# Odd attention's values product over pairs of token tiles in split parts, with the head norm taken over partitions

## The chip, the cores and the metric

The kernel runs on one core of a Trainium2 chip. The metric is the time of one execution on the device in microseconds. Five engines have instruction queues of their own: TensorE (PE), VectorE (DVE), ScalarE (ACT), GpSimd (POOL) and SyncE (SP, which issues transfers here). PE's weight loads are listed as PEld.

## The reference

A bidirectional encoder of two layers is applied to a prompt of 256 tokens and a sample of 512 tokens, width 1024, with shared weights. The even layer has neighbourhood and grouped-query attention, the odd layer differential attention with 8 heads; an MLP follows each. The change lies in the odd layer:

```python
def diff_attention(q, k, v, lam):
    ...
        s = jnp.einsum('bqhcd,bkhcd->bhcqk', q_blk, kk).astype(jnp.float32) * scale
        p = jax.nn.softmax(s, axis=-1)
        a = (p[:, :, 0] - lam * p[:, :, 1]).astype(v.dtype)
        return jnp.einsum('bhqk,bkhe->bqhe', a, v)
...
            o = diff_attention(qc, kc, vc, lam)
            o = rmsnorm(o, subln_g[j], SUBLN_EPS) * (1.0 - lam_init)
            x = x + o.reshape(B, T, DIFF_WIDTH) @ w_out_o[j]
```

For each head there are two score maps (64 features each); the second softmax, times lambda, is taken from the first. The difference multiplies values of 128 features, and the result is normalized over those 128 features for each token.

## The kernel before

Both requests lie side by side as 768 tokens, six tiles of 128; tiles 0 to 3 are the sample (512 keys), tiles 4 and 5 the prompt (256 keys). Large products are done in split form: each f32 operand is written as a high part in the type F32R and the remainder as a low part (`wsplit`, `halve`; ACT writes the high part, DVE subtracts), and three F32R products, high-high, high-low and low-high, are added in PSUM.

Odd attention is a pipeline of two strands that share the PE queue. The first is a chain of projection steps: `proj_v` (values of two heads, tokens in the partitions) and `proj_qk` (queries and keys of one head, then the rotary products on DVE `t`, L697, the sum on POOL `rope_o`, L705 and L706, and a transpose on PE with split evacuation, `put_T`), and at the end `out_proj`. One step is six matmuls over 256 columns, in `out_proj` three over 512 and three over 256. The second strand is 48 attention units, one for each head `h` and token tile `t` (`diff_unit`), with four parts:

- `f_s`: six score matmuls into two PSUM tiles (L278), for each map the maximum `m` on DVE (L727) and the exponential `de` on ACT (L729), then on DVE the reciprocals `ri`, the factor `cf`, and the weighted sum of both maps (L734), not yet divided by the first map's sum.
- `f_t`: transposes of that sum on PE (L288), copied to SBUF by DVE and ACT in turn (L292, L294).
- `f_v`: the values product in plain f32, tokens in the partitions (L744); `od` on ACT divides by the first map's sum; ACT squares with a sum over the free axis (`odq`, L749), DVE makes the mean `ss`, POOL takes the power -0.5 (`rn`, L752), DVE multiplies (`o_tok`, L754).
- `f_o`: a PE transpose `otp` (L299) and a copy by ACT into the head's tile `do`, features in the partitions.

`attention` and `ramp` set the order in which the strands are written down: the units of head h lie between given steps of the chain, 36 steps for a full head, and in unit i come `f_s(i)`, half of the steps, `f_o(i-2)`, `f_v(i-1)`, the other half, `f_t(i)`. A scheduler that goes by priority and its own estimates of readiness sets the final order on each engine; each engine then works in that order. PSUM has three banks with the tag `mm` (projections) and five with the tag `at` (scores, transposes, values).

The even layer's grouped-query attention has a class `Values` that takes two token tiles together: transposes of both into one PSUM bank, split evacuation `gph` (L456, L457), and matmuls over 256 columns with features in the partitions.

Of the kernel before, what the change touches and what calls it, by code (L numbers as in the profile page):

```python
# [11 lines left out]
F32 = mybir.dt.float32  # L12
# [25 lines left out]
def kernel(ctx: ExitStack, tc: tile.TileContext, a: dict, y: bass.AP):  # L38
# [13 lines left out]
    nc.vector.memset(ones, 1.0)  # L52
    nhalf = cpool.tile([P, 8], F32, name="nhalf")
# [10 lines left out]
    def ps_tile(tag, name):  # L64
        return psum.tile([P, 512], F32, tag=tag, name=name, bufs=BANKS[tag])
# [214 lines left out]

    flip = [0]

    def transposed(pool, blocks, tag, name):

        n = len(blocks)
        pt = ps_tile("at", f"{name}_ps")
        for i, b in enumerate(blocks):
            nc.tensor.transpose(out=pt[:, i * P : (i + 1) * P], in_=b, identity=ident)  # L288
        sb = pool.tile([P, 512], F32, tag=tag, name=name)
        flip[0] ^= 1  # L290
        if flip[0]:
            nc.vector.tensor_copy(sb[:, : n * P], pt[:, : n * P])  # L292
        else:
            nc.scalar.activation(sb[:, : n * P], pt[:, : n * P], AF.Copy)  # L294
        return sb

    def o_out(o_tok, o_tile, t, gain=1.0):
        pt = ps_tile("at", "otp")[:, :P]
        nc.tensor.transpose(out=pt, in_=o_tok, identity=ident)  # L299
        nc.scalar.activation(o_tile[:, t * P : (t + 1) * P], pt, AF.Copy, scale=gain)  # L300
# [6 lines left out]
    def xo_tile(name):  # L307
        return xpool.tile([P, NT], F32, tag="xo", name=name, bufs=9)
# [335 lines left out]
    def odd_attention(xs, nm, sg, spill):  # L644
# [17 lines left out]
        def proj_v(n):  # L662
            col = wgroup("w_in_o")
            v = vs[n] = ap.tile([P, TT, 256], F32, tag="v", name=f"dv{n}", bufs=2)
            pend = []
            for t in range(TT):
                ps = ps_tile("mm" if n or t < 3 else "at", "dvp")
                yield from proj_tok(col, xs, t, ps)
                pend.append((t, ps))
                if not rts and t == 3:  # L670
                    rts.append(nm.rstd())
                while rts and pend:
                    t_, ps = pend.pop(0)
                    nc.scalar.activation(v[:, t_, :], ps[:, :256], AF.Copy, scale=rts[0][:, t_ : t_ + 1])
# [10 lines left out]
        def proj_qk(h):  # L685
            col = wgroup("w_in_o")
            d = qks[h] = [ap.tile([P, 2, NT], F32R, tag="qk", name=f"d{h}_{i}", bufs=6) for i in range(2)]
# [20 lines left out]

        def diff_unit(h, t):
            if t == 0:  # L710
                o[h] = xo_tile("do")
            d = qks[h]
            v, o_tile = vs[h // 2], o[h]
            vc = slice((h % 2) * P, (h % 2) * P + P)
# [5 lines left out]
            st = {}  # L720

            def f_s():
                es_ = []
                ss = scores("ds", nk * P, lambda i, hp, s: d[i][hp, 0, s], lambda i, hp, s: d[i][hp, 1, s], tk, ks)
                for c, s in enumerate(ss):
                    m = spool.tile([P, 1], F32, tag="m", name="m")
                    nc.vector.tensor_reduce(out=m, in_=s, axis=AX.X, op=ALU.max, negate=True)  # L727
                    e = ap.tile([P, 512], F32, tag="e", name="de", bufs=4)[:, : nk * P]
                    nc.scalar.activation(e, s, AF.Exp, bias=m, scale=1.0, accum_out=l2[:, c : c + 1])  # L729
                    es_.append(e)  # L730
                nc.vector.reciprocal(ri, l2)
                cf = spool.tile([P, 1], F32, tag="cf", name="cf", bufs=2)
                nc.vector.scalar_tensor_tensor(out=cf, in0=ri[:, 1:2], scalar=l2[:, 0:1], in1=neglam, op0=ALU.mult, op1=ALU.mult)
                nc.vector.scalar_tensor_tensor(out=es_[0], in0=es_[1], scalar=cf, in1=es_[0], op0=ALU.mult, op1=ALU.add)  # L734
                st["e"] = es_[0]

            def f_t():
                st["pt"] = transposed(ap, [st["e"][:, i * P : (i + 1) * P] for i in range(nk)], "pt", "dpt")

            def f_v():  # L740
                pt = st["pt"]
                pv = ps_tile("at", "dpv")[:, :P]
                for i in range(nk):
                    nc.tensor.matmul(pv, pt[:, i * P : (i + 1) * P], v[:, k0 // P + i, vc], start=(i == 0), stop=(i == nk - 1))  # L744
                od = ap.tile([P, P], F32, tag="od", name="od", bufs=2)
                nc.scalar.activation(od, pv, AF.Copy, scale=ri[:, 0:1])
                sq = ap.tile([P, P], F32, tag="odq", name="odq", bufs=1)
                ss = spool.tile([P, 1], F32, tag="ss", name="ss")
                nc.scalar.activation(sq, od, AF.Square, accum_out=ss)  # L749
                nc.vector.tensor_scalar(ss, ss, 1.0 / P, 1e-5, op0=ALU.mult, op1=ALU.add)  # L750
                rn = spool.tile([P, 1], F32, tag="rn", name="rn")
                nc.gpsimd.tensor_tensor(out=rn, in0=ss, in1=nhalf[:, :1], op=ALU.pow)  # L752
                st["o"] = ap.tile([P, P], F32, tag="o_tok", name="o_tok", bufs=2)
                nc.vector.tensor_scalar(st["o"], od, rn[:, 0:1], None, op0=ALU.mult)  # L754

            def f_o():
                o_out(st["o"], o_tile, t, sg[:, 0:1])

            return f_s, f_t, f_v, f_o
# [563 lines left out]
```

## Time and profile before

| what | value |
|---|---|
| median of three runs | 1723.32 us (1722.27 to 1725.19) |
| profiled execution | 1722.56 us, span 1720.8 us |
| TensorE clock granted, mean | 0.996 |
| busy over the span: PE, PEld, DVE, ACT, POOL | 99%, 94%, 78%, 52%, 21% |
| odd attention, with its projections | from 833 to 1208 us of the span |

Busy is the share of the span in which an engine executed something; it doesn't count the time in which a queue stands because its next instruction waits for another engine. Waits are listed apart, with the engine and line that ended them. The profiled execution lies 0.8 us under the median.

### The profile page before, as it was taken

The page shows a single profiled execution, that of the slowest core. Times are in us where ns is not written, and L with a number is a line of the kernel's source. Part 1 is how long each engine was busy: PE and PEld are TensorE (multiplying, and loading weights), DVE is VectorE, ACT ScalarE, POOL GpSimd, SP SyncE. Part 2 cuts the span into 40 slices and gives each one's busy share as a digit, 9 for nine tenths or more (in the row PEclk, how much of TensorE's full clock was granted, in tenths as well). Part 3 has the DMA queues.
Part 4 walks back from the last instruction along what each step waited for, and adds up shares of the span by engine and source line. Part 5 has one row for each costly group of instructions (what it writes and reads, how often), then busy time and mean ns, then how long its engine had stood idle before and what let it go on. Part 6 is the DMA issues. An engine that isn't in the chain of part 4 may idle for free. (4 is left out here: it accounts for less than half of the span.)

```text
span 1720.8 us, 28225 instructions
## 1 busy us (share of the span) xinstructions
PE 1695.1 (99%) x10844; PEld 1610.7 (94%) x10844; DVE 1344.5 (78%) x2356; ACT 897.1 (52%) x1617; POOL 355.5 (21%) x380
## 2 busy tenths in 40 slices
PE   8999999999999999999999999999999999999997
PEld 8888888899999999999999999988999999999997
DVE  8888779798887787878676776776898776878785
ACT  7765656464554544444445555555545554544442
POOL 2200000116555200000021222210246554000001
PEclk9999999999999999999999999999999999999998
DMA  5111223315544688653310111112145445996521
GB/s 172 38 47 50 68 81 107 123 53 187 169 170 163 228 311 321 218 160 131 131 50 26 50 40 33 56 59 86 50 164 175 160 169 192 331 322 228 190 90 74
DMA packets 74598, 235.42 MB, mean 137 GB/s; under 512 B 7904, under 2 KB 25056, under 8 KB 74464
## 3 DMA queue, kind: packets, MB, share of 16 engines
q1 hardware_dynamic: 52480, 186.93, 32.8%
q0 software_dynamic: 7168, 25.17, 4.3%
q10 hardware_dynamic: 14816, 21.52, 3.5%
q8 instruction: 85, 1.39, 0.3%
q14 instruction: 49, 0.40, 0.1%
HBM read 182.47 MB, written 50.33 MB: 135 GB/s over the span
## 5 line engine op out<-in xcount | busy, mean ns | idle before, releaser
L883 PE MATMUL up<-c,whi 128*128 128x384 f32 x1808 | 464.8, 338 | 1.2 <-ACT c L122 0.6
L1082 PE MATMUL dn<-th,whi 128*128 128x384 f32 x1792 | 462.2, 339 | 3.8 <-DVE th L120 3.8
L1082 PEld LDWEIGHTS dn<-th,whi 128*128 128x128 f32 x1792 | 326.9, 188 | 4.4 <-DVE th L120 4.4
L883 PEld LDWEIGHTS up<-c,whi 128*128 128x128 f32 x1808 | 328.2, 188 | 2.7 <-ACT c L122 1.3
L883 PE MATMUL up<-c,wlo 128*128 128x384 f32 x904 | 305.2, 338 | 0.0
L1082 PE MATMUL dn<-th,wlo 128*128 128x384 f32 x896 | 303.3, 339 | 0.0
L83 ACT ACTIVATE whi<-ch 128x1024 fp32r<-128x1024 f32 x88 | 93.2, 1062 | 179.4 <-PE dn L1082 164.8
L868 POOL TENSOR_TENSOR s<-wraw 128x512 f32<-128x512 f32 x60 | 93.2, 1569 | 449.5 <-DMA wraw<-in_w_up_dram 360.1
L883 PEld LDWEIGHTS up<-c,wlo 128*128 128x128 f32 x904 | 169.7, 188 | 0.0
L1082 PEld LDWEIGHTS dn<-th,wlo 128*128 128x128 f32 x896 | 168.9, 189 | 0.0
L83 ACT ACTIVATE whi<-wraw 128x1024 fp32r<-128x1024 f32 (+3 forms) x128 | 116.6, 911 | 89.0 <-PE up L883 62.9
L84 DVE TENSOR_TENSOR wlo<-ch,whi 128x1024 fp32r<-128x1024 f32 x88 | 107.1, 1223 | 56.6 <-ACT whi L83 55.2
L84 DVE TENSOR_TENSOR wlo<-wraw,whi 128x1024 fp32r<-128x1024 f32 (+3 forms) x132 | 138.9, 1052 | 14.0 <-ACT whi L83 13.8
L83 ACT ACTIVATE whi<-s 128x1024 fp32r<-128x1024 f32 x60 | 63.7, 1062 | 127.6 <-PE up L883 118.2
L200 PE MATMUL dqk<-whi,xh 128*128 128x256 f32 x384 | 114.8, 299 | 0.0
L171 POOL TENSOR_TENSOR rt<-ms,nhalf 128x6 f32<-128x6 f32 (+1 forms) x6 | 9.0, 1492 | 501.8 <-DVE ms L170 501.8
L200 PE MATMUL dqk<-whi,xl 128*128 128x256 f32 x384 | 107.4, 280 | 0.0
L200 PE MATMUL dqk<-wlo,xh 128*128 128x256 f32 x384 | 107.2, 279 | 0.0
L84 DVE TENSOR_TENSOR wlo<-s,whi 128x1024 fp32r<-128x1024 f32 x60 | 84.1, 1402 | 23.1 <-ACT whi L83 22.9
L120 DVE TENSOR_TENSOR th<-tr,th 128x1536 fp32r<-128x1536 f32 x56 | 98.2, 1753 | 3.5 <-ACT th L119 3.4
L729 ACT ACTIVATE de<-ds,m 128x512 f32<-128x512 f32 (+1 forms) x96 | 58.3, 612 | 81.3 <-DVE m L727 81.3
L891 DVE TENSOR_TENSOR z<-up,z 128x384 f32<-128x384 f32 x180 | 96.6, 550 | 1.0
(235 smaller groups left out, 3765.8 us busy)
## 6 DMA issues: line engine op xcount, KB each, us to landing
wd<-in_w_down_dram SPq DMA_DIRECT2D x84, 512.0 KB, 4.8
tr<-T SPq DMA_DIRECT2D x56, 768.0 KB, 5.7
wraw<-in_w_up_dram SPq DMA_DIRECT2D x64, 512.0 KB, 3.7
T<-t POOLq DMA_DIRECT2D x64, 384.0 KB, 3.1
T<-z ACTq DMA_DIRECT2D x32, 576.0 KB, 3.0
ch<-in_w_down_dram SPq DMA_DIRECT2D x28, 512.0 KB, 5.1
wraw<-in_w_in_o_dram SPq DMA_DIRECT2D x24, 512.0 KB, 3.6
wraw<-in_w_in_e_dram SPq DMA_DIRECT2D x16, 512.0 KB, 3.6
```

What stands on the lines that cost most here:

```text
L83: nc.scalar.activation(hi, raw, AF.Copy)
L84: nc.vector.tensor_tensor(out=lo, in0=raw, in1=hi.bitcast(F32), op=ALU.subtract)
L120: nc.vector.tensor_tensor(out=lo, in0=src, in1=hi.bitcast(F32), op=ALU.subtract)
L171: nc.gpsimd.tensor_tensor(out=rt, in0=ms, in1=nhalf[:, :n], op=ALU.pow)
L200: nc.tensor.matmul(ps[:, :256], st[:, tk], col(k, part, 0, 256), start=(k == 0 and i == 0), stop=(k == KD - 1 and i == 2))
L729: nc.scalar.activation(e, s, AF.Exp, bias=m, scale=1.0, accum_out=l2[:, c : c + 1])
L868: nc.gpsimd.tensor_tensor(out=d_, in0=x_, in1=y_, op=ALU.add)
L883: nc.tensor.matmul(ps, part[a_][:, base + k * P : base + (k + 1) * P], t[:, b_], start=start and k + i == 0, stop=stop and k == 3 and i == 2)
L891: nc.vector.tensor_tensor(out=out, in0=x_, in1=y_, op=op)
L1082: nc.tensor.matmul(ps, w[a_][:, c : c + P], th[:, b_, q], start=i + q + a_ + b_ == 0, stop=i == NG - 1 and q == ND - 1 and a_ == 1)
```

## The change

The attention units keep their places, but from `f_t` on they work on pairs of neighbouring token tiles (0 and 1, 2 and 3, 4 and 5) of a head. The weighted sum of the two maps is now fully normalized before it is transposed: ACT multiplies the second map by `cf`, DVE multiplies the first by its reciprocal sum and adds. A pair's transposes are taken in parts of two key blocks (two parts over 512 keys, one over 256), each part evacuated as a high and a low half. The values are kept as high and low halves also, and the product is done as three split products over 256 tokens, with the features in the partitions. The norm's sum over features is a product with a 128 by 128 matrix of ones, in two parts (high and low of the squares): each partition then holds the sums of all 256 tokens. DVE transposes that in blocks of 32 by 32, so that 8 columns hold the 256 sums; mean, epsilon and power are taken on these 8 columns, and a second block transpose from a broadcast spreads them again over the partitions. One DVE instruction multiplies and writes the head's output tile; the output transposes on PE are gone. The q/k tiles have four instead of six buffers.

```diff
+    ones_r = cpool.tile([P, P], F32R, name="ones_r")
+    nc.scalar.activation(ones_r, ident, AF.Copy, scale=0.0, bias=1.0)
...
-            v = vs[n] = ap.tile([P, TT, 256], F32, tag="v", name=f"dv{n}", bufs=2)
+            v = vs[n] = ap.tile([P, TT, 2, 256], F32R, tag="v", name=f"dv{n}", bufs=2)
...
-                    nc.scalar.activation(v[:, t_, :], ps[:, :256], AF.Copy, scale=rts[0][:, t_ : t_ + 1])
+                    r = rts[0][:, t_ : t_ + 1]
+                    nc.scalar.activation(v[:, t_, 0], ps[:, :256], AF.Copy, scale=r)
+                    nc.vector.scalar_tensor_tensor(out=v[:, t_, 1], in0=ps[:, :256], scalar=r, in1=v[:, t_, 0].bitcast(F32),
+                                                   op0=ALU.mult, op1=ALU.subtract)
...
+        class Values:
+            def __init__(self, h, t):
+                self.o, self.tk = o[h], slice(t * P, t * P + 256)
+                self.k0, self.nk = (0, 4) if t < 4 else (4, 2)
+                self.v, self.vc = vs[h // 2], slice((h % 2) * P, (h % 2) * P + P)
+                self.parts = list(range(0, self.nk, 2))
+                self.es, self.live, self.od = [], [], None
+
+            def turn(self):
+                if not self.parts:
+                    return
+                i = self.parts.pop(0)
+                pt = ps_tile("at", "dpt_ps")
+                for b in range(2):
+                    for t in range(2):
+                        nc.tensor.transpose(out=pt[:, b * 256 + t * P : b * 256 + (t + 1) * P],
+                                            in_=self.es[t][:, (i + b) * P : (i + b + 1) * P], identity=ident)
+                hl_ = ap.tile([P, 2, 512], F32R, tag="pt", name="dph", bufs=2)
+                nc.scalar.activation(hl_[:, 0], pt, AF.Copy)
+                nc.vector.tensor_tensor(out=hl_[:, 1], in0=pt, in1=hl_[:, 0].bitcast(F32), op=ALU.subtract)
+                self.live.append((i, hl_))
+
+            def values(self):
+                if self.parts or not self.live:
+                    return
+                pv = ps_tile("at", "dpv")[:, :256]
+                for i, hl_ in self.live:
+                    for b in range(2):
+                        for part, mv in ((0, 0), (0, 1), (1, 0)):
+                            nc.tensor.matmul(pv, self.v[:, self.k0 + i + b, part, self.vc], hl_[:, mv, b * 256 : (b + 1) * 256],
+                                             start=i + b + part + mv == 0, stop=i + b == self.nk - 1 and part == 1)
+                self.live = []
+                ...
+                nc.scalar.activation(self.ms, pv, AF.Square)
+                nc.scalar.activation(self.sq[:, 0], self.ms, AF.Copy)
+                nc.vector.tensor_tensor(out=self.sq[:, 1], in0=self.ms, in1=self.sq[:, 0].bitcast(F32), op=ALU.subtract)
+                nc.scalar.activation(self.od, pv, AF.Copy)
+
+            def out(self):
+                if self.od is None:
+                    return
+                ss = ps_tile("at", "dss")[:, :256]
+                for part in range(2):
+                    nc.tensor.matmul(ss, ones_r, self.sq[:, part], start=part == 0, stop=part == 1)
+
+                nc.vector.transpose(self.ms, ss)
+                m8 = spool.tile([P, 8], F32, tag="m8", name="m8", bufs=2)
+                nc.vector.tensor_scalar(m8, self.ms[:, 0:256:32], 1.0 / P, 1e-5, op0=ALU.mult, op1=ALU.add)
+                nc.gpsimd.tensor_tensor(out=m8, in0=m8, in1=nhalf, op=ALU.pow)
+                nc.vector.transpose(self.ms.rearrange("p (b t) -> p b t", t=32), m8[:, :, None].broadcast_to([P, 8, 32]))
+                nc.vector.scalar_tensor_tensor(out=self.o[:, self.tk], in0=self.od, scalar=sg[:, 0:1], in1=self.ms,
+                                               op0=ALU.mult, op1=ALU.mult)
+                self.od = None
...
+            if t % 2 == 0:
+                vals.append(Values(h, t))
+                del vals[:-2]
+            v = vals[-1] if t % 2 else vals[0] if len(vals) > 1 else None
+            now = vals[-1]
...
-                nc.vector.scalar_tensor_tensor(out=cf, in0=ri[:, 1:2], scalar=l2[:, 0:1], in1=neglam, op0=ALU.mult, op1=ALU.mult)
-                nc.vector.scalar_tensor_tensor(out=es_[0], in0=es_[1], scalar=cf, in1=es_[0], op0=ALU.mult, op1=ALU.add)
-                st["e"] = es_[0]
...
+                nc.vector.tensor_tensor(out=cf, in0=ri[:, 1:2], in1=neglam, op=ALU.mult)
+                nc.scalar.activation(es_[1], es_[1], AF.Copy, scale=cf)
+                nc.vector.scalar_tensor_tensor(out=es_[0], in0=es_[0], scalar=ri[:, 0:1], in1=es_[1], op0=ALU.mult, op1=ALU.add)
+                now.es.append(es_[0])
+
+            return f_s, lambda: v and v.turn(), lambda: v and v.values(), lambda: v and v.out()
```

The old `f_t`, `f_v` and `f_o` of `diff_unit` go, with their helpers `transposed` and `o_out`. The exponentials' buffers, four of one tag, become three for the first map and one for the second.

More of the change, by code (lines that the diff above doesn't have):

```diff
@@ L279, in scores @@
         return out
[L281 to L300, printed above, removed]
     def ramp(marks):
@@ L686, in proj_qk @@
             col = wgroup("w_in_o")
-            d = qks[h] = [ap.tile([P, 2, NT], F32R, tag="qk", name=f"d{h}_{i}", bufs=6) for i in range(2)]
+            d = qks[h] = [ap.tile([P, 2, NT], F32R, tag="qk", name=f"d{h}_{i}", bufs=4) for i in range(2)]
             for t in range(TT):
@@ L707, in proj_qk @@
                 chain.later(7, lambda o=o, t=t: put_T(o, d, t))
+        class Values:
[28 more added lines that the diff above has]
+                self.live = []
+                self.ms = ap.tile([P, 256], F32, tag="ms", name="dms", bufs=1)
+                self.od = ap.tile([P, 256], F32, tag="od", name="od", bufs=1)
+                self.sq = ap.tile([P, 2, 256], F32R, tag="odq", name="odq", bufs=1)
+                nc.scalar.activation(self.ms, pv, AF.Square)
[16 more added lines that the diff above has]
+                self.od = None
@@ L709, in diff_unit @@
+        vals = []
         def diff_unit(h, t):
@@ L711, in diff_unit @@
                 o[h] = xo_tile("do")
+            if t % 2 == 0:
[3 more added lines that the diff above has]
+            now = vals[-1]
             d = qks[h]
-            v, o_tile = vs[h // 2], o[h]
-            vc = slice((h % 2) * P, (h % 2) * P + P)
             tk = slice(t * P, (t + 1) * P)
@@ L719, in diff_unit @@
             ri = spool.tile([P, 2], F32, tag="ri", name="ri")
-            st = {}
             def f_s():
@@ L727, in f_s @@
                     nc.vector.tensor_reduce(out=m, in_=s, axis=AX.X, op=ALU.max, negate=True)
-                    e = ap.tile([P, 512], F32, tag="e", name="de", bufs=4)[:, : nk * P]
+                    e = ap.tile([P, 512], F32, tag=f"e{c}", name="de", bufs=(3, 1)[c])[:, : nk * P]
                     nc.scalar.activation(e, s, AF.Exp, bias=m, scale=1.0, accum_out=l2[:, c : c + 1])
@@ L732, in f_s @@
                 cf = spool.tile([P, 1], F32, tag="cf", name="cf", bufs=2)
-                nc.vector.scalar_tensor_tensor(out=cf, in0=ri[:, 1:2], scalar=l2[:, 0:1], in1=neglam, op0=ALU.mult, op1=ALU.mult)
-                nc.vector.scalar_tensor_tensor(out=es_[0], in0=es_[1], scalar=cf, in1=es_[0], op0=ALU.mult, op1=ALU.add)
-                st["e"] = es_[0]
[L737 to L759, printed above, removed]
+                nc.vector.tensor_tensor(out=cf, in0=ri[:, 1:2], in1=neglam, op=ALU.mult)
[3 more added lines that the diff above has]
+            return f_s, lambda: v and v.turn(), lambda: v and v.values(), lambda: v and v.out()
         o = [None] * 8
```

## The prediction

> **What bounds the kernel now.** I read the page's busy shares first, then the table of windows for the stage, the waits of PE and of DVE, and then single rows. PE is the engine that is full, DVE the next.
>
> ```profile
> PE 1695.1 (99%) x10844; PEld 1610.7 (94%) x10844; DVE 1344.5 (78%) x2356; ACT 897.1 (52%) x1617; POOL 355.5 (21%) x380
> 833.00:1208.00 375.00, 373.66 (x2947) 341.80 (x2946) 257.89 (x672) 191.09 (x529) 78.95 (x146) 1.00 0.18 57
> 920.00:1000.00 80.00, 80.00 (x665) 74.15 (x664) 56.49 (x158) 43.63 (x128) 19.29 (x36) 1.00 0.14 41
> 1000.00:1080.00 80.00, 80.00 (x664) 74.15 (x663) 56.48 (x158) 43.62 (x127) 19.29 (x36) 1.00 0.13 39
> 48.00:95.00 47.00, 46.97 (x331) 39.68 (x331) 41.70 (x117) 34.60 (x106) 10.63 (x16) 1.00 0.16 47
> ```
>
> The window rows read: stretch, length, then PE, weight load, DVE, ACT, POOL busy, PE clock, DMA share, GB/s. Odd attention with its projections is 833 to 1208; PE is busy in 373.66 of 375 us there at full clock. The stretches 920 to 1000 and 1000 to 1080 are two heads each (the same counts and busy times recur): 40.0 us a head, DVE 28.2 us of it. The last row, the grouped-query attention of the even layer, is my reference for a loaded DVE: 89% busy and PE still full.
>
> ```profile
> PE opa L212 <- DVE ol L120: 0.7, 1, 0.7
> PE opb L212 <- DVE x L792: 0.3, 1, 0.3
> PE otp L299 <- ACT dpt L294: 0.3, 1, 0.3
> PE up L883 <- DVE c L123: 0.3, 1, 0.3
> PE up L883 <- ACT c L122: 0.2, 1, 0.2
> ```
>
> These are all of PE's waits from 830 to 1240: 1.8 us. So PE's own issue sets the time of the stage now, and whatever PE instructions go are gained, unless another queue then takes longer than PE. That queue would be DVE's, in-order; its waits from 920 to 1120 (five heads) are:
>
> ```profile
> DVE o_tok L754 <- POOL rn L752: 22.6, 30, 1.5
> DVE ri L731 <- ACT de L729: 15.6, 19, 0.9
> DVE ss L750 <- ACT odq L749: 6.9, 9, 1.8
> DVE t L697 <- PE dqk L200: 4.4, 9, 0.5
> DVE m L727 <- PE ds L278: 3.7, 7, 1.2
> DVE dpt L292 <- PE dpt_ps L288: 0.7, 2, 0.3
> ```
>
> The first two lines are no slack: DVE has sent work to POOL or ACT and stands until it comes back, 4.5 and 3.1 us a head. Slack is only what waits in the end for PE (the last four, 15.7 us, 3.1 a head). So DVE is used for 40.0 − 3.1 = 36.9 us of each head, though its busy share says 71%.
>
> **The change part by part: PE.** Pace of the matmuls, from starts in the timeline:
>
> ```profile
> 885.83 0.28 PE L200 MATMUL dqk<-whi,xl 128*128 128x256 f32 x1
> 885.95 1.05 PE L744 MATMUL dpv<-dv,dpt 128*128 128x128 f32 x8
> 886.75 0.36 PE L200 MATMUL dqk<-whi,xh 128*128 128x256 f32 x1
> 886.96 0.28 PE L200 MATMUL dqk<-wlo,xh 128*128 128x256 f32 x1
> 887.07 0.28 PE L200 MATMUL dqk<-whi,xl 128*128 128x256 f32 x1
> 1187.18 0.27 PE L299 MATMUL otp<-ident,o_tok 128*128 128x128 f32 x1
> 1187.29 1.06 PE L744 MATMUL dpv<-dv,dpt 128*128 128x128 f32 x8
> ```
>
> A split matmul over 256 columns starts every 0.118 us. The old product of one token tile over 512 keys (four f32 matmuls, eight records) holds PE 0.80 us, and the split matmul behind it takes 0.21 instead of 0.118: 0.89 in all; over 256 keys half the records, 0.45. The output transpose adds 0.11. Old, a head: 4 × (0.89 + 0.11) + 2 × (0.45 + 0.11) = 5.12 us. New: two pairs of tiles with 12 matmuls and one with 6, and three times two matmuls with the ones: 36 × 0.118 = 4.25 us. Score transposes stay 20 a head; in larger groups, taken at nothing. PE saves 0.87 us a head, 7.0 us in all: a head would take 39.1 us.
>
> [...]
>
> **DVE.** Durations for old and new instructions:
>
> ```profile
> L457 DVE TENSOR_TENSOR gph<-gpt_ps,gph x40: 671/682/693, 62.9 to 182.4; 128x512 fp32r<-128x512 f32 x40
> L292 DVE COPY dpt<-dpt_ps 128x512 f32<-128x512 f32 x16 | 10.9, 684 | 0.6 <-PE dpt_ps L288 0.6
> L292 DVE COPY dpt<-dpt_ps 128x256 f32<-128x256 f32 x8 | 3.4, 422 | 2.7 <-PE dpt_ps L288 2.7
> L734 DVE SCALAR_TENSOR_TENSOR de<-de,cf 128x256 f32<-128x256 f32 x16 | 7.7, 482 | 0.4
> L683 DVE TENSOR_TENSOR d<-dqkT,d 128x256 fp32r<-128x256 f32 x48 | 20.0, 417 | 6.0 <-ACT d L682 6.0
> L510 DVE TENSOR_SCALAR ge<-ge,ri 128x256 f32<-128x256 f32 x5 | 1.8, 354 | 0.2
> L754 DVE TENSOR_SCALAR o_tok<-od,rn 128x128 f32<-128x128 f32 x48 | 13.9, 291 | 33.8 <-POOL rn L752 33.7
> L750 DVE TENSOR_SCALAR ss<-ss 128x1 f32<-128x1 f32 x48 | 7.1, 149 | 15.9 <-ACT odq L749 15.5
> ```
>
> Back to back, one instruction starts about 0.08 us before the last has ended (the timeline's pairs of L457 take 1.29 us), so I take 0.08 off each except where it waits for its predecessor. Removed a head: half of the copies of the transposed scores (2 × 0.60 + 0.34), six `ss` (0.90), six `o_tok` (6 × 0.21): 3.7 us. Added: five low parts of the scores by L457 (5 × 0.62 = 3.1); the low part of V, three tiles by L683 (1.0); for each of three pairs the low part of the squares (0.34), the block transpose from PSUM (0.42, by the 256-wide copy), `m8` (0.15), the transpose back (0.35, by L510) and the final product (0.40, by L734): 1.66 × 3 = 5.0. Together 9.1, net +5.4: busy 28.2 becomes 33.6 us a head. `cf` and the weighted sum keep their prices.
>
> No row here shows a block transpose. I bound the pair between 0.5 us (both as narrow operations like `o_tok`) and 1.6 us (each twice its 256-wide neighbour) and take 0.77, that of the same-width copies. [...]
>
> **The waits that DVE's queue holds.** The power on POOL moves from 128x1 six times a head to 128x8 three times, and DVE's second transpose stands behind it:
>
> ```profile
> 1189.28 0.15 DVE L750 TENSOR_SCALAR ss<-ss 128x1 f32<-128x1 f32 x1 [0.52 <-ACT odq L749]
> 1189.57 0.55 POOL L752 TENSOR_TENSOR rn<-ss,nhalf 128x1 f32<-128x1 f32 x1 [4.96 <-DVE ss L750]
> 1190.16 0.29 DVE L754 TENSOR_SCALAR o_tok<-od,rn 128x128 f32<-128x128 f32 x1 [0.73 <-POOL rn L752]
> L57 POOL TENSOR_TENSOR one<-ones,nhalf 128x8 f32<-128x8 f32 x1 | 1.7, 1660 | 1.5 <-ACT nhalf L54 1.5
> L752 POOL TENSOR_TENSOR rn<-ss,nhalf 128x1 f32<-128x1 f32 x48 | 26.3, 549 | 161.5 <-DVE ss L750 161.5
>   POOL rn L752: 33.7, 47
> ```
>
> The last row is from the answer on the tile `od`: waits in us, and how many. The setup's 128x8 power took 1.66 us. With the handovers (0.11 beyond the power itself in most of the old cases) DVE is held 1.77 us a pair, 5.3 a head, against 4.5 before. What is queued behind it is the rotary products (which free the projection's PSUM banks), the maxima of the next scores and the low parts: all that PE comes back for. The scheduler put at most one other instruction, a rotary product, between `ss` and `o_tok`, and 47 of 48 `o_tok` waited for the power; so I let it fill 0.3 us a pair and take 4.4 us a head.
>
> A new hand-over: the second map is scaled by `cf` on ACT, and the weighted sum on DVE waits for it.
>
> ```profile
> L294 ACT ACTIVATE dpt<-dpt_ps 128x512 f32<-128x512 f32 x16 | 9.6, 598 | 13.7 <-PE dpt_ps L288 13.6
> L278 PE MATMUL gs<-gk,gq x144: 271/392/503, 48.1 to 176.0; 64*128 64x512 f32 x96, 64*128 64x256 f32 x48
> DVE ri L509 <- ACT ge L506: 2.0, 4, 1.1
> ```
>
> By the first row it takes some 0.6 us, six times a head, 3.9 us with handovers if nothing fills it. The second row gives the even layer's rhythm (six score matmuls a unit, 24 units from 48.1 to 176.0, one in 5.6 us); the third is the exponential's wait there in the stretch 48 to 95, where DVE was 89% busy: 2.0 us over some eight units, 0.25 each, against 0.52 a unit in odd attention (15.6 over 30). A fuller queue fills such gaps. So for exponential and `cf` together 12 × 0.25 = 3.0 us a head; the far ends are 0 and 3.1 + 3.9 = 7.0.
>
> ACT gains 5 copies of 0.6, six scalings, and three wider steps a pair, and loses `od`, `odq`, `do` and its share of copies: net about +1.5 us a head on 21.8, no bound. V's doubled tile and four instead of six q/k buffers: the second head's writes begin after the head two before has been read, no wait.
>
> **The sum.** DVE a head: 33.6 + 4.4 + 3.0 = 41.0; with about 1 us of waiting for PE that remains when two queues are this close (it is 3.1 now), 42.0, against PE's 39.1 and today's 40.0. So DVE sets the pace: +2.0 us a head over seven heads, +14. The eighth runs beside the output projection, where the two effects about cancel. At the very end the chain from the last ones product to the last output is 0.42 + 0.15 + 1.77 + 0.35 + 0.48 = 3.2 us, behind six steps of the projection; between 0 and 2 us, I take 0. The profiled execution took 1722.56 us, span 1720.8 and 1.8 around it, 0.8 below the median of the runs: 1722.6 + 14 = 1736.6, rounded to 1736.
>
> **The rivals.** (1) Faster: PE stays the bound. The mechanism is the saving of 7.0 us, and it decides if DVE's sum stays below 39.1, that is if the power's gap and the two ACT gaps together cost under 5.5 us a head instead of 7.4. For it: the stretch 48 to 95 with DVE at 89% and PE full; 33.6 of 39.1 is 86%. Against: no power stands in DVE's way there. Price: 1722.6 − 7.0, and 1 of new stalls: 1716.6. (2) Level: DVE lands at 39.5 to 40.5 us a head, 1719.5 to 1726. (3) The gaps aren't filled at all: 33.6 + 5.3 + 7.0 + 1 = 46.9, +6.9 a head, 1771; the exponential's unfilled 0.82 us in 19 of 30 cases speaks for it, the fuller queue against. Block transposes at 1.6 a pair would add 2.5 us a head, 1754.
>
> **How the numbers follow.** A measurement here tells about 0.2%, 3.4 us. DVE as the bound 0.54 (own range 1727 to 1756, with 0.08 beyond it for the third rival), level 0.16, PE as the bound 0.30. The range runs from 1715, PE's full saving, to 1754, leaving some 0.15 out. Faster 0.30, same 0.16, slower 0.54.
>
> **What would show it.** Right: PE idle of several us a head within the stage, released by DVE (rotary products, low parts, score tiles); DVE's second transpose waiting some 1.7 us for the power; DVE busy plus those waits near 100%. The output transposes gone and `dpv` matmuls at 0.118. Wrong: PE still full from 876 to 1200 with the stage 7 us shorter; or other work standing between `m8` and the second transpose; or block transposes far from 0.4 us.

## The result and the profile after

The changed kernel takes 1747.8 us (median of 4 runs, 1741.95 to 1749.82) against 1722.86 (1722.27 to 1725.19): ratio 1.0136, 95% interval 1.0124 to 1.0147. The forecast was 1736.0, slower, with 1715 to 1754 as its range.

The profiled execution took 1749.82 us, span 1748.0. The stage from the first matmul of V's projection (`dvp`) to the first of the next MLP (`up`), by the starts in PE's timeline, was 391.2 us before (834.1 to 1225.3) and is 420.2 after (833.7 to 1253.8): +29.0. The rest of the span is 1.8 us shorter. So the loss lies wholly in this stage. The same stage is named for every experiment below, because the part ahead of it, at which no edit is aimed, ends anywhere from 828.6 to 834.2 us.

The page's busy shares of the changed kernel:

```profile
PE 1699.9 (97%) x10764; PEld 1609.3 (92%) x10764; DVE 1392.9 (80%) x2420; ACT 909.3 (52%) x1562; POOL 374.7 (21%) x356
```

PE went from 99% to 97%, DVE from 78% to 80%. By shares alone DVE isn't overloaded. A window of the changed kernel (stretch, length, PE, weight load, DVE, ACT, POOL busy, PE clock, DMA share, GB/s):

```profile
920.00:1120.00 200.00, 183.61 (x1426) 165.37 (x1426) 152.86 (x390) 102.69 (x249) 55.03 (x69) 0.97 0.12 36
```

Before, PE was busy in all of the 160 us from 920 to 1080, at clock 1.00. Now it has holes, and the clock isn't full either. The largest of PE's waits, 820 to 1260:

```profile
PE dpt_ps L711 <- DVE de L783: 20.0, 11, 3.0
```

The holes are nearly all at one place (the next largest wait is 1.3 us): the transposes of the weighted scores (L711) wait for DVE's weighted sum (L783), 11 times, up to 3.0 us. What DVE does ahead of one of the long ones, from its timeline (start, duration, instruction, idle before it and who ended that):

```profile
1016.36 0.15 DVE L781 TENSOR_TENSOR cf<-ri,neglam 128x1 f32<-128x1 f32 x1
1016.43 0.44 DVE L744 STREAM_TRANSPOSE dms<-dss 128x256 f32<-128x256 f32 x1
1016.91 0.18 DVE L746 TENSOR_SCALAR m<-dms 128x8 f32<-128x8 f32 x1
1019.11 0.45 DVE L748 STREAM_TRANSPOSE dms<-m 128x256 f32<-128x256 f32 x1 [2.03 <-POOL m L747]
1019.48 0.71 DVE L783 SCALAR_TENSOR_TENSOR de<-de,ri 128x512 f32<-128x512 f32 x1
```

`cf` is the factor that ACT needs to scale the second map, and while ACT does that the scheduler has filled DVE's queue with the norm of an earlier pair: block transpose, `m8`, and the transpose back. That last one has to wait for POOL's power, and the weighted sum, ready long before, stands behind it in the in-order queue. The chain of the changed kernel, 1012 to 1022, shows that this is what the transposes hang on there:

```profile
1017.43 1.66 POOL m L747
...
1019.11 0.45 DVE dms L748
1019.56 0.65 DVE de L783
...
1020.25 0.55 PE dpt_ps L711 x3
```

This order explains the longest of the 11 waits, not all of them. Of the 24 second block transposes only four lie between a `cf` and its weighted sum, with 7.8 of the 34.8 us that DVE stands for the power; they are ahead of the waits that end at 930.71, 1020.25, 1108.74 and 1198.41, 10.9 of the 20.0 us. Ahead of the other seven DVE's queue holds rotary products, first block transposes, low parts of weights and projections, or a stand for the exponential or for ACT's scaling.

The waits of DVE, 920 to 1120, all that are over 1.7 us:

```profile
DVE dms L748 <- POOL m L747: 19.7, 14, 2.0
DVE ri L779 <- ACT de L777: 9.5, 17, 0.9
DVE de L783 <- ACT de L782: 3.6, 10, 0.8
DVE d L667 <- ACT d L666: 3.2, 4, 1.5
DVE dv L657 <- ACT dv L656: 2.1, 2, 1.0
DVE odq L733 <- ACT odq L732: 1.9, 4, 0.6
DVE dph L715 <- ACT dph L714: 1.8, 4, 0.7
```

Not one of them is for PE, for which DVE waited 8.8 us in the same stretch before: nearly all of that slack is gone. And the prices of the new operations, from the groups of 833 to 1235 (busy, mean ns of one, idle before):

```profile
L747 POOL TENSOR_TENSOR m<-m,nhalf 128x8 f32<-128x8 f32 x24 | 46.3, 1930 | 140.2 <-DVE m L746 135.9 <-DVE cf L781 4.0
L748 DVE STREAM_TRANSPOSE dms<-m 128x256 f32<-128x256 f32 x24 | 10.7, 445 | 34.8 <-POOL m L747 34.8
L744 DVE STREAM_TRANSPOSE dms<-dss 128x256 f32<-128x256 f32 x24 | 10.6, 443 | 1.7 <-PE dss L742 1.4
```

PE's own saving came as forecast. By the starts in the timeline, 12 split matmuls hold PE 1.44 us, 6 hold it 0.71, two ones products 0.24 where nothing holds them up: 2 × 1.44 + 0.71 + 3 × 0.24 = 4.31 us a head. The old product with its output transpose held it 4 × 1.005 + 2 × 0.558 = 5.14. That is 0.83 us a head, 6.6 in all, against 0.87 and 7.0.

So the bill of the stage is: PE's visible waits from 1.3 to 23.1 us (+21.8), the matmul saving (−6.6), stretches at half clock (at most +7.6, last section), and 6 us or more that lie hidden within PE's records. Part of these: six of the 22 pairs of ones products that run back to back held PE 0.68 to 0.70 us, the others 0.23 to 0.32; in the six the load of the second half of the squares waited for DVE's low part, 0.3 us each.

### The profile page after: what moved, and what is told of

It is laid out like the page before. It is cut to its first block, busy times and chain, and to the rows that moved or that the text cites. A ratio compares the mean times of both kernels' runs of the same rounds, so it can differ in the third digit from the quotient of the medians.

```text
span 1748.0 us, 28016 instructions
## 1 busy us (share of the span) xinstructions
PE 1699.9 (97%) x10764; PEld 1609.3 (92%) x10764; DVE 1392.9 (80%) x2420; ACT 909.3 (52%) x1562; POOL 374.7 (21%) x356
## 4 chain that ended last, share of the span: by engine, by line
PE 80%; DVE 8%; ACT 3%; POOL 3%; issue 3%; DMA 2%; POOLq 0%; SPq 0%; ACTq 0%
PE dn L1109 26%; PE up L910 25%; PE dqk L202 4%; PE opa L214 3%; PE npa L214 3%; PE dvp L202 2%; POOL m L747 2%; PE vp L202 2%; PE opb L214 2%; PE qp L202 2%; PE gs L280 1%; PE npb L214 1%; ACT de L777 1%; DVE wlo L86 1%; PE gpv L450 1%
## 5 line engine op out<-in xcount | busy, mean ns | idle before, releaser
L86 DVE TENSOR_TENSOR wlo<-wraw,whi 128x1024 fp32r<-128x1024 f32 (+3 forms) x132 | 137.6, 1043 | 10.4 <-ACT whi L85 10.2
```

The costliest lines, as they stand in the source:

```text
L86: nc.vector.tensor_tensor(out=lo, in0=raw, in1=hi.bitcast(F32), op=ALU.subtract)
```

## The experiments

Four theories are tested, with the letters of the recorded expectations. Theory A: DVE stands for the 128x8 power on POOL, with the weighted sum and other work for PE queued behind. Theory B: the new hand-over, ACT's scaling of the second map, makes the chain to the transposes too long. Theory C: DVE has too much *work*, so that any order loses. Theory D: the single buffers `ms` and `od` make ACT wait for DVE and so hold the next pair up. A and B can hold together.

All results in one table. Each ratio, with its 95% interval, is to executions of the kernel before that were taken beside that run, so it isn't always the median shown divided by 1722.86. Stage, PE's gaps in it and its time at half clock are those of the profiled execution:

| run | median us | ratio | stage us | PE gaps us | half clock us |
|---|---|---|---|---|---|
| before | 1722.86 | 1 | 391.2 | 1.3 | 0 |
| after | 1747.80 | 1.0136 (1.0124 to 1.0147) | 420.2 | 23.1 | 17.1 |
| e1_short_pow | 1724.58 | 1.0002 (0.9987 to 1.0017) | 396.8 | 9.6 | 3.4 |
| e2_no_hand | 1735.85 | 1.0063 (1.0041 to 1.0085) | 406.0 | 14.6 | 0 |
| e3_light | 1748.66 | 1.0121 (1.0083 to 1.0159) | 418.7 | 22.6 | 13.7 |
| e4_bufs2 | 1751.82 | 1.0156 (1.0135 to 1.0178) | 422.3 | 24.1 | 27.3 |
| e5_short_nohand | 1720.95 | 0.9985 (0.9970 to 1.0000) | 390.7 | 4.4 | 0 |
| e6_defer | 1725.56 | 1.0012 (1.0001 to 1.0024) | 396.8 | 8.9 | 0 |
| e7_defer_dvs | 1724.52 | 1.0017 (1.0006 to 1.0028) | 396.1 | 11.7 | 0 |
| e8_before_hand | 1728.91 | 1.0038 (1.0023 to 1.0053) | 396.6 | 3.4 | 0 |
| e9_late | 1737.49 | 1.0084 (1.0070 to 1.0099) | 413.7 | 16.1 | 13.7 |
| e10_before_pow8 | 1753.91 | 1.0177 (1.0152 to 1.0202) | 427.5 | 23.9 | 10.2 |
| e11_late2 | 1743.69 | 1.0106 (1.0087 to 1.0125) | 418.9 | 22.2 | 13.7 |
| e12_defer_nohand | 1723.15 | 0.9991 (0.9978 to 1.0004) | 394.5 | 7.4 | 0 |

A microsecond at half clock costs at most 0.45 (0.118 against 0.213 us from matmul to matmul, last section). So up to 7.6 us of the changed kernel's stage, and part of what a run gains or loses against it, is the clock.

### e1_short_pow: the power on one column

```diff
-                nc.gpsimd.tensor_tensor(out=m8, in0=m8, in1=nhalf, op=ALU.pow)
-                nc.vector.transpose(self.ms..., m8[:, :, None].broadcast_to([P, 8, 32]))
+                nc.gpsimd.tensor_tensor(out=m8[:, :1], in0=m8[:, :1], in1=nhalf[:, :1], op=ALU.pow)
+                nc.vector.transpose(self.ms..., m8[:, :1, None].broadcast_to([P, 8, 32]))
```

> The changed kernel, but the power on POOL is taken on one of the 8 columns only (0.55 us by the kernel before instead of 1.93 us), and that column is spread to all tokens; the norm of the other 7/8 of the tokens is left out. All engines keep their order of instructions. Theory A (DVE stands for the wide power, and the weighted sum that PE's transposes need is queued behind it): each of 24 stands shortens by up to 1.4 us; most of PE's 24 us of waits and its half-clock windows go: 1718 to 1728 us. Theory B (the new hand-over of the second map to ACT makes the chain to the transposes too long): little changes, 1740 to 1750. Theory C (DVE has simply too much work): little changes in its busy time, so 1738 to 1750.

Ratio 1.0002: the whole loss is gone. PE, DVE, ACT and POOL have the instructions of the changed kernel in the same order; only the power's width differs. Its mean fell from 1.93 to 0.84 us. Waits of PE and of DVE, 820 to 1260:

```profile
PE dpt_ps L711 <- DVE de L783: 8.6, 9, 1.6
```

```profile
DVE dms L748 <- POOL m L747: 9.9, 17, 0.9
```

DVE's stand fell by 24.9 us (34.8 to 9.9) and the stage by 23.4, of which up to 6.1 is the half clock that went with it (17.1 to 3.4 us). Theory A holds.

### e2_no_hand: no scaling on ACT

```diff
-                nc.vector.tensor_tensor(out=cf, in0=ri[:, 1:2], in1=neglam, op=ALU.mult)
-                nc.scalar.activation(es_[1], es_[1], AF.Copy, scale=cf)
-                nc.vector.scalar_tensor_tensor(out=es_[0], in0=es_[0], scalar=ri[:, 0:1], in1=es_[1], ...)
+                nc.vector.scalar_tensor_tensor(out=cf, in0=ri[:, 1:2], scalar=l2[:, 0:1], in1=neglam, ...)
+                nc.vector.scalar_tensor_tensor(out=es_[0], in0=es_[1], scalar=cf, in1=es_[0], ...)
```

> The changed kernel, but the second map is not scaled on ACT: factor and weighted sum on DVE as in the kernel before, so the division by the first map's sum is left out (the norm behind it takes it away but for its epsilon). DVE's busy time stays as it is. Theory A: the power still holds DVE; 1738 to 1748. Theory B: ACT's scaling (0.72 us, 48 times) and its handover go from the chain; PE's waits go, 1718 to 1728. Theory C: as A, 1740 to 1750.

Ratio 1.0063: about half of the loss goes with the hand-over. 1735.85 us lies between what was expected under A and under B. Waits of PE and of DVE, 820 to 1260:

```profile
PE dpt_ps L711 <- DVE de L782: 7.1, 9, 1.6
```

```profile
DVE dms L748 <- POOL m L747: 36.6, 24, 1.8
```

DVE stands for the power as long as ever (36.6 us), yet PE waits a third as long at the score transposes. As I read it, the weighted sum no longer sits on the far side of a trip to ACT, so the stand less often falls between `cf` and it: once in the stage (1.7 us) instead of four times. The two causes don't add: e1 alone takes away 23.4 us of stage, e2 alone 14.2, of 29.0. That fits two links of one chain; part of both is half clock that is no longer there.

### e3_light: less work for DVE, everything else kept

```diff
-                    nc.vector.scalar_tensor_tensor(out=v[:, t_, 1], in0=ps[:, :256], ...)      # low part of V
-                nc.vector.tensor_tensor(out=self.sq[:, 1], in0=self.ms, ...)                   # low part of the squares
```

(the matmuls read the high parts in their stead)

> The changed kernel without two of DVE's new operations, the low parts of V and of the squares (0.47 us each, 48 in all, 22.6 us of DVE's busy time); the high parts are used in their place, so PE's matmuls are all there; the low parts' terms are left out. The power and the hand-over stay. Theory C (DVE's work as such): 2.8 us a head come back, 1722 to 1732 us. Theories A and B (what stands in the chain): 1738 to 1748.

Ratio 1.0121: no gain that the intervals can tell from the changed kernel. Windows of e3:

```profile
920.00:1120.00 200.00, 185.74 (x1446) 168.07 (x1445) 143.10 (x366) 103.33 (x252) 55.75 (x70) 0.97 0.12 36
```

and its DVE waits over the same stretch:

```profile
DVE dms L745 <- POOL m L744: 19.1, 14, 1.8
DVE ri L776 <- ACT de L774: 12.1, 17, 0.9
DVE dph L713 <- ACT dph L712: 9.9, 12, 2.6
DVE d L665 <- ACT d L664: 6.7, 5, 2.3
DVE de L780 <- ACT de L779: 4.7, 11, 0.8
```

This is the run to hold against e1. The removed instructions were 22.6 us of DVE's time in the stage (24 of 0.468 and 24 of 0.474), the shorter power took 24.9 us of DVE's standing. The first moved the stage by 1.5 us, the second by 23.4. DVE did the less work and then waited the longer: for `dph` 9.9 us where it was 1.8, for `d` 6.7 where it was 3.2; and PE still waited 15.0 us at the score transposes. So Theory C falls as the main account of this loss. It isn't as clean as the sum over the stage looks: from the second start of V's projections to the fourth (four heads) e3 was 5.7 us shorter than the changed kernel, up to 3.0 of that by less half clock there (3.4 us against 10.2), and behind the fourth it was 4.3 us longer again, with 3.7 us of waits of PE at the output projection instead of 1.3.

### e4_bufs2: two buffers for `ms` and `od`

```diff
-                self.ms = ap.tile([P, 256], F32, tag="ms", name="dms", bufs=1)
-                self.od = ap.tile([P, 256], F32, tag="od", name="od", bufs=1)
+                self.ms = ap.tile([P, 256], F32, tag="ms", name="dms", bufs=2)
+                self.od = ap.tile([P, 256], F32, tag="od", name="od", bufs=2)
```

(room for them from setup tiles of the stage that share other tags)

> The changed kernel with two buffers in place of one for the squares' tile and the product's copy (room for them from small setup tiles). ACT waited 20.6 us, 7 times, for the final product of the pair before, once a head. Theory D (ACT held there delays what PE waits for): PE's waits shrink, 1730 to 1740 us. Theories A, B and C: that wait stands off the chain, 1742 to 1750.

Ratio 1.0156. ACT's waits for the final product of the pair before, 20.6 us in the changed kernel, are gone, but PE still waits 21.1 us at the score transposes and nothing is gained, though up to 4.6 us of the time is the longer half clock (27.3 us against 17.1): Theory D falls.

### e5_short_nohand: e1 and e2 together

> Both takings-away together: the power on one column only (the norm of 7/8 of the tokens left out) and the second map not scaled on ACT (the division by the first map's sum left out). If the power's stand and the hand-over are the two causes and lie in one chain, PE's waits in the stage go down to the 2 us of the kernel before and the PE saving shows whole: 1714 to 1719 us. If DVE's work as such keeps PE waiting, it stays at 1722 to 1728.

Ratio 0.9985, at the edge of what can be told from no change. Windows of e5, then its DVE waits over 920 to 1120, then PE's over 820 to 1260:

```profile
920.00:1120.00 200.00, 197.93 (x1603) 181.72 (x1602) 167.51 (x442) 97.44 (x250) 50.46 (x81) 1.00 0.12 39
```

```profile
DVE ri L779 <- ACT de L777: 13.1, 22, 0.9
DVE dms L748 <- POOL m L747: 6.5, 13, 0.7
DVE odq L733 <- ACT odq L732: 4.2, 6, 1.3
DVE dv L657 <- ACT dv L656: 2.4, 2, 1.2
DVE d L667 <- ACT d L666: 2.0, 4, 0.6
DVE dph L715 <- ACT dph L714: 1.3, 4, 0.4
```

```profile
PE dpt_ps L711 <- DVE de L782: 2.6, 6, 0.6
```

With both links taken out PE is full again, 197.93 of 200 us. Against e2, which has the same instructions in the same order on PE, DVE, ACT and POOL and no half clock either, only the power's width differs: DVE's stand went from 36.6 to 10.7 us and the stage from 406.0 to 390.7. So 25.9 us less of standing were worth 15.3 us, 0.6 for one, though in e2 only 1.7 us of it stood between a `cf` and its sum: a stand costs at other places of DVE's queue too. The time expected if both were the whole cause, 1714 to 1719 us, was missed: the stage is 390.7 us, 0.5 under before, though PE has 6.6 us less to do, and 3.1 came back as visible gaps. DVE's busy time and these waits are 197.0 of the 200 us; that its queue now runs level with PE's and hides the saving fits this and wasn't tested.

### e6_defer and e7_defer_dvs: the second transpose behind the weighted sum

The full computation. In e6 the second transpose and the final product go out half a unit later, held in DVE's queue behind the last weighted sum (`after[0]`); `ms` and `od` have two buffers. In e7 DVE also does ACT's scaling.

```diff
+                def rest():
+                  with tc.issue_after(getattr(after[0], "ins", after[0])):
                     nc.vector.transpose(self.ms..., m8[:, :, None].broadcast_to([P, 8, 32]))
                     nc.vector.scalar_tensor_tensor(out=self.o[:, self.tk], in0=od, ...)
+                late.append(rest)
...
+            return (f_s, lambda: (v and v.turn(), flush()), lambda: v and v.values(),
+                    lambda: (flush(), v and v.out(), ...))
```

> The whole computation, reordered: the second block transpose and the final product are written half a unit later and held behind the weighted sum of the unit in between on DVE (two buffers for the squares and the product's copy, as in the run before with these alone). The power runs while DVE does other work. Theory A: the stand goes out of the chain that PE waits for; 1722 to 1732 us, what is left being the hand-over. If DVE's order had nothing to do with it: 1745 to 1752.

> The reordered kernel, and the scaling of the second map moved from ACT to DVE (0.48 instead of 0.72 us and no handover, but some 20 us more DVE work in the stage); the whole computation is done. If the chain's length decides: 1716 to 1724 us. If DVE's work decides: slower than the run with the reordering alone, 1730 and above.

Ratios 1.0012 and 1.0017. Waits of e6, PE and DVE, 820 to 1260:

```profile
PE dpt_ps L711 <- DVE de L794: 7.0, 8, 1.5
```

```profile
DVE dms L752 <- POOL m L747: 18.2, 16, 1.8
```

With the power at its full width and all work in, another *order* gives back 23.4 us of the stage's 29.0, up to 7.6 of it as half clock that is gone. That is Theory A without leaving anything out, though place and length aren't told apart: no second transpose is left between a `cf` and its sum, and DVE's stand for the power also fell, from 34.8 to 18.2 us. In e7 DVE has 48 instructions more than in e6 and ACT 48 fewer, and the time is the same within the intervals; 1724.52 us is just over the 1724 expected if the chain decides, and well under the 1730 expected if DVE's work does.

### e8_before_hand and e10_before_pow8: each cause alone in the kernel before

```diff
-                nc.vector.scalar_tensor_tensor(out=es_[0], in0=es_[1], scalar=cf, in1=es_[0], ...)
+                nc.scalar.activation(es_[1], es_[1], AF.Copy, scale=cf)
+                nc.vector.scalar_tensor_tensor(out=es_[0], in0=es_[1], scalar=ones[:, 0:1], in1=es_[0], ...)
```

```diff
-                rn = spool.tile([P, 1], F32, tag="rn", name="rn")
-                nc.gpsimd.tensor_tensor(out=rn, in0=ss, in1=nhalf[:, :1], op=ALU.pow)
+                rn = spool.tile([P, 8], F32, tag="rn8", name="rn", bufs=2)
+                nc.gpsimd.tensor_tensor(out=rn, in0=ss.broadcast_to([P, 8]), in1=nhalf, op=ALU.pow)
```

(e8 above, e10 below; both compute what the kernel before does)

> The kernel before with the hand-over alone: ACT multiplies the second map by the factor, DVE adds it to the first; nothing else changes. If the hand-over alone makes the chain too long: 1728 to 1738 us. If the kernel before has the slack to hide 0.8 us a unit and only the sum of both additions breaks it: 1722 to 1725.

> The kernel before with the power taken on 8 columns in place of one (seven are copies and unused), 48 times: DVE stands some 1.4 us longer a unit in front of the product with the norm, nothing else changes. If a stand of DVE reaches the transposes of the next unit: 1740 to 1765 us. If the kernel before can hide it: 1722 to 1726.

The trip to ACT alone costs 1.0038, the wide power alone 1.0177. In e10 PE, DVE, ACT and POOL keep the order of before. Its waits, DVE and PE, 820 to 1260:

```profile
DVE o_tok L754 <- POOL rn L752: 89.6, 48, 2.6
```

```profile
PE dpv L744 <- DVE dpt L292: 6.5, 7, 1.6
PE otp L299 <- DVE o_tok L754: 4.2, 6, 1.4
PE dpt_ps L288 <- DVE de L734: 3.8, 6, 0.8
```

The stand grew from 33.7 to 89.6 us, and the stage by 36.3, up to 4.6 of it by half clock. Here the delay came out at three kinds of PE work, none dominant. Some 0.6 of a longer stand became time even in a kernel whose DVE had slack by its busy share (78%).

### e9_late and e11_late2: score transposes one unit later

To give the weighted sum time, `turn` moves one unit back, so that the first map needs four buffers (e9) and the norm comes half a unit (e9) or a unit (e11) after the values.

```diff
-            v = vals[-1] if t % 2 else vals[0] if len(vals) > 1 else None
+            v = vals[-2] if len(vals) > 1 else None
...
-                    e = ap.tile([P, 512], F32, tag=f"e{c}", name="de", bufs=(3, 1)[c])[:, : nk * P]
+                    e = ap.tile([P, 512], F32, tag=f"e{c}", name="de", bufs=(4, 1)[c])[:, : nk * P]
```

> The whole computation with every operation of the changed kernel, moved in time: the transposes of a pair are written a unit later (with the pair before), so that the weighted sum has a whole unit more before PE needs it (four buffers in place of three for the first map, room from small setup tiles); the norm follows the values product after half a unit. DVE's and ACT's work, the wide power and the hand-over all stay. If the length of the chain in front of the transposes is the cause, PE's waits go and most of its 7 us show: 1713 to 1720 us. If DVE's time in total is the cause: 1735 to 1750.

> As the run with the transposes a unit later, but the norm keeps its old distance of one unit behind the values product, and the last head keeps the changed kernel's order: both chains that PE came upon too early (weighted sum to transposes, squares to ones product) now have a unit. All operations, the wide power and the hand-over stay. If those two distances are all that was wrong: PE waits in the stage under 6 us and 1714 to 1721 us. If DVE, standing for the power 35 us in the stage, is short of time as well, the waits turn up at another place and it stays at 1725 and above.

Ratios 1.0084 and 1.0106. From the waits of e9, then of e11, PE, 820 to 1260:

```profile
PE dss L746 <- ACT odq L736: 8.0, 7, 1.3
PE dpt_ps L711 <- DVE de L788: 1.3, 1, 1.3
```

```profile
PE dss L742 <- ACT odq L732: 7.9, 6, 1.8
PE dpv L725 <- DVE dph L715: 4.6, 7, 1.7
PE dqkT L664 <- POOL rope_o L690: 4.6, 5, 1.3
PE dpt_ps L711 <- DVE de L783: 1.9, 1, 1.9
```

The wait at the score transposes went from 20.0 to under 2 us, as meant, and PE then waited at the ones product, the values and the projection's transposes. DVE still stood 33.0 and 40.2 us for the power. Both times lie where the expectations put them for a DVE short of time (1735 to 1750, and 1725 and above), not where the distance to the transposes alone would have: that distance wasn't all. DVE's operations as such aren't what is too much either, since e6 has the same ones and takes 1725.56 us. What differs is the order, and with it the stands: 33.0 and 40.2 us here, 18.2 there. Giving one consumer more time didn't help much while the stands stayed.

### e12_defer_nohand: e6 without ACT's scaling

> The kernel of e6 (second transpose and final product half a unit later, behind the weighted sum) with ScalarE's scaling of the second map taken out as well: VectorE makes the factor from both sums and the weighted sum in one instruction, as before the change. Left out is the division of a head's values by its first map's sum, which the norm over features takes out again but for its epsilon. The wide power stays at 128x8. If the two stands of VectorE ahead of the weighted sum (for the power, and for ScalarE's hand-over) are what the change costs, taking both away without shortening the power leaves TensorE's own saving of 0.84 us a head: waits of the score transposes for the weighted sum at 3 us or less in the stage, ratio 0.995 to 0.999 (1714 to 1721 us). If VectorE is short of time in any order, the deferred transposes only wait at another place and the ratio is 1.000 to 1.003 (1722 to 1728 us), with TensorE's waits moved to the values' or the sums' buffers.

Ratio 0.9991 (0.9978 to 1.0004), between the ratios of the two outcomes expected. The waits at the score transposes were 4.7 us, over the 3 named, and the stage 3.3 us longer than before. DVE still stands 25.8 us for the power, three quarters of the 34.8, none of it between a `cf` and its sum, and the loss is gone; but PE's saving doesn't come through. Neither e5 nor e12 is told from the kernel before; no version here beats both kernels by what can be measured. What wasn't run is e5 with less work for DVE, which would say whether PE's 6.6 us show up once the queue has slack again.

## Why the prediction was right, and where it wasn't

DVE's account per head, in the form of the prediction. A head takes 44.1 us (half the mean distance of V's projections two heads apart, which start at 892.1, 980.0 and 1068.5), so the 200 us from 920 to 1120 hold 4.535 heads; e3 and e5 in the same way (892.5, 976.1, 1063.2: 42.7 us; 887.0, 966.4, 1046.3: 39.8 us), each from its window row and waits shown above:

| us a head | forecast | after | e3 | e5 |
|---|---|---|---|---|
| DVE busy | 33.6 | 33.7 | 30.5 | 33.4 |
| stands for the power | 4.4 | 4.3 | 4.1 | 1.3 |
| stands for exponential and scaling | 3.0 | 2.9 | 3.6 | 2.6 |
| **sum of these** | **41.0** | **40.9** | **38.2** | **37.3** |
| waits for `d`, `dv`, `odq`, `dph` from ACT | – | 2.0 | 3.5 | 2.0 |
| rest | 1.0 | 1.2 | 0.9 | 0.6 |
| **a head** | **42.0** | **44.1** | **42.7** | **39.8** |

- **PE's saving:** 0.87 forecast, 0.83 measured. Right, and never seen whole in any run's time.
- **DVE's instructions:** the block transposes were taken at 0.42 and 0.35 us, between 0.5 and 1.6 for the pair; they took 0.443 and 0.445. The low parts of V and of the squares took 0.468 and 0.474, a little over the 0.417 of the row that they were priced by. None of it moved the sum: 33.7 against 33.6.
- **The power:** 1.93 us in the mean, not 1.66. It was 1.64 or 1.65 in 16 of 24 cases and 2.2 to 2.7 in the other eight. The eight were partly covered by other DVE work, so the stand came out at 4.3 a head all the same.
- **The hand-over and the exponential:** 2.9 a head where 3.0 was taken; the far end, 7.0, is excluded. The scaling itself, taken at 0.6, took 0.72 us over 512 keys and 0.51 over 256.
- **The step that failed is the remainder, "about 1 us of waiting".** It is 3.2 a head. 2.0 of it are waits for ACT's other results (`d`, `dv`, `odq`, `dph`), to which the sum gave no term; before, the only one of that kind among the rows shown was the odq wait, 1.4 a head, and the prediction called it slack, which waits in the end for PE, though its row names ACT. That is 4.1 instead of 2.0 over the 40.0 of before. How much of the excess comes from the half clock stays open: 920 to 1120 holds 10.2 us of it, worth at most 1.0 a head. Seven heads at 4.1 make 28.7 us, near the stage's 29.0, but that the eighth adds nothing is shown by no run: by the starts of V's projections four heads took 16.9 us more, the rest of the stage behind them 14.4 more, and the part ahead of them 2.3 less.
- **"DVE sets the pace" was right as to the engine, and its rule was wrong.** The sum came out at 40.9 against 41.0, and still the prediction's rule, a head takes DVE's sum and about 1, fails where the sum changes: in e3 the sum fell by 2.7 and the head by 1.4, as waits for ACT grew by 1.5; in e5 it fell to 37.3, under PE's 39.1, and the head took 39.8. A stand proved dearer than work: 0.6 of each microsecond became time where only the stand changed and the clock stayed full (e5 against e2), where e3's work off the same queue was worth 1.5 of 22.6 us over the stage. The forecast came near because both terms stood in one sum; that the time fell within the range is in part luck, for the increase was nearly twice the one forecast (24.9 us against 13). Why work taken away comes back as waits for ACT is not shown.
- **What would show it:** the second transpose waiting for the power came, 34.8 us over 24 cases in the stage, 1.45 each against the 1.7 named. DVE busy plus waits near 100% came: 152.86 + 41.8 of 200, 97%. PE's idle time, released by DVE, came too, but at the transposes of the weighted scores, which the list didn't name; rotary products, low parts and score tiles were not where it waited. The output transposes are gone, and the values matmuls run at 0.12 us each (12 in 1.44).
- **Rival 1** (PE stays the bound) was to decide if the power's gap and the two ACT gaps cost under 5.5 us a head; they cost 7.2. In e5 they cost 3.9, and still the head took 39.8, not 39.1, so the condition wasn't enough. **Rival 2** (level, 39.5 to 40.5 a head) isn't what the changed kernel did, at 44.1, but where e5 landed. **Rival 3** (gaps unfilled, 46.9 a head) is excluded by the same rows. The forecast also rounded its own 1736.6 down to 1736.
- **The half clock** was in no step; it is worth up to 7.6 us of the stage.

## What to carry to other kernels

An engine that works in order and sends work away should have the instruction that collects the result queued *behind* whatever feeds the bound engine. Here 24.9 us of standing taken away were worth 23.4 us of the stage (at least 17 without the clock), 25.9 us in another pair of runs 15.3, and 22.6 us of plain work taken off the same queue 1.5. When many instructions change, look for what the new wait stands in front of, before adding up busy time. And when two engines are within a few per cent of each other, don't count on a saving on one of them: PE's 6.6 us never came out.

## What the runs showed of the hardware that was not expected

**Half clock after gaps of 1.6 to 3 us.** After the gap of 3.01 us that ended at 930.71 PE ran at half clock, and after that of 3.00 which ended at 1020.25 as well. Windows of the changed kernel, cut at the second place:

```profile
1022.00:1025.40 3.40, 3.40 (x19) 3.40 (x18) 2.28 (x6) 1.74 (x5) 0.87 (x2) 0.51 0.00 0
1025.40:1028.80 3.40, 3.40 (x28) 2.83 (x28) 2.47 (x7) 1.40 (x3) 0.81 (x2) 1.00 0.00 0
```

The clock column goes from 0.51 to 1.00: PE is busy throughout both stretches and has 19 matmuls in the first, 28 in the second. Split matmuls there start every 0.213 us instead of 0.118. The clock records have four such stretches in the stage, three of 3.413 us and one of 6.827, 17.07 in all, and their starts lie whole multiples of 3.413 us apart (92.16 = 27 times, 129.71 = 38 times, 47.79 = 14 times). At 0.118 in place of 0.213 that is at most 7.6 us lost, less where PE waited as well. Besides the two gaps of 3.0 us, gaps of 2.18 and 1.91 us (ended at 1150.08 and 1198.41) were followed by it as well, and one of 1.58 us in e1 (ended at 924.91). So a stall can cost more than its length: the 3.413 us at half clock behind the gap of 1.91 us were worth up to 1.5 us more, by the same two paces.

The length of a gap doesn't tell alone: one of 2.99 us, ended at 1108.74, brought no half clock. PE's busy time in stretches of 3.41 us of the same phase, first the one ahead of the half clock at 1021.95, then the two across which that gap lies (stretch, length, PE busy, clock, DMA share, GB/s):

```profile
1018.54:1021.95 3.41, 1.70 (x11) 1.00 0.00 0
1103.87:1107.28 3.41, 1.88 (x15) 1.00 0.16 63
1107.28:1110.69 3.41, 1.95 (x13) 1.00 0.00 0
```

Ahead of the other three half-clock stretches PE was busy for 1.32, 1.57 and 1.50 us of 3.41. So in this stage half clock began where PE had been idle for 1.71 us or more of such a stretch, and not after one with 1.53 or less. That is no limit for all runs: in e9 it followed stretches in which PE was busy for 2.05 to 2.40 us.

**The power slows beside the low part of a weight.** Two powers of the changed kernel, from POOL's timeline, and DVE's timeline at the first:

```profile
1008.61 2.60 POOL L747 TENSOR_TENSOR m<-m,nhalf 128x8 f32<-128x8 f32 x1 [11.00 <-DVE m L746]
1017.43 1.65 POOL L747 TENSOR_TENSOR m<-m,nhalf 128x8 f32<-128x8 f32 x1
```

```profile
1008.48 1.22 DVE L86 TENSOR_TENSOR wlo<-wraw,whi 128x1024 fp32r<-128x1024 f32 x1
```

At 1008.61, under the low part of a weight (`wlo`), the power took 0.95 us longer than at 1017.43, where DVE stood still. All eight of the slow powers (2.2 to 2.7 us) overlap a `wlo`, and none of the 16 at 1.64 or 1.65 does. Why is not shown. The weighted sum at 1009.63 ran under the same power and took 0.75 us, the median of the 28 of its shape that met no power, so it was not slowed. The slow powers didn't set the stalls shown: those had the 1.65.
